# Moving two decay tiles of each group into the group ahead, the diagonal products behind a projection, and dt's sums behind another chunk

## The chip, the cores and the metric

The kernel runs on one core of a Trainium2 chip. A core has TensorE (matrix products, into PSUM), VectorE, ScalarE and GpSimd (POOL), which run their own instruction queues in order, and a SyncE queue (SP) whose only work here is to issue DMA transfers. The metric is the time of one execution in microseconds; lower is better.

## The reference, cut to what matters

Two layers run over 128 context tokens and 512 latent tokens: gated attention (layer 0), and a bidirectional Mamba-2 scan (layer 1), which the change touches. Of layer 1:

```
proj = h @ w_in                       # -> z, xbc, dt
xbc  = silu(conv3(xbc) + b)           # -> xs (2048), bs, cs (4 groups x 128)
dt   = softplus(dt + bias)            # 32 heads forward, 32 backward
a_cs = cumsum(a * dt)                 # within a chunk of 128 tokens; backward from the end
decay = exp(where(lower, a_cs[l] - a_cs[s], -inf))
y_diag = ((c @ b.T) * decay) @ (xs * dt)
states = b.T @ (xs * dt * exp(a_cs[-1] - a_cs))
h      = h * exp(a_cs[-1]) + states   # from chunk to chunk, both directions
y      = y_diag + (c @ h_prev) * exp(a_cs) + d_skip * xs
out    = rms_norm(y * silu(z)) @ w_out
```

There are 5 token tiles of 128 (tile 0 is the context, tiles 1 to 4 the latent tokens), and 32 heads in 4 groups of 8.

## The kernel before, in words

Layer 1 starts with a projection for dt (`dt_stage`, L917), a generator that is resumed between the first projections. Its first part projects; the second makes softplus on VectorE in a chain of small dependent operations that ends in L957 to L960; the third makes the running sums with two small products (L966, L967) and a total (L972); the fourth transposes the sums (L982) and stores them to DRAM in 40 small DMAs, one for each tile, group and direction (L990), and their exponential in one (L994).

Then `layer1` goes through 4 groups (g) of 10 steps (j). In a step stand the scan's operations of group g and, from the table `fl`, projections for what comes later. `x_unit` projects and convolves one chunk of 128 channels of xs for group g + 1 (48 products, L914, then VectorE's L1001, L1002, L1003, ScalarE's tanh L1005, VectorE's L1006), `bc_unit` does the same for B and C, `z_unit` projects a chunk of the gate path. `x_turn` and `b_turn` transpose a convolved chunk (L1014). In the last group, projections of the output (`part_mm`, L1380) stand in their place. A projection's result stands in the PSUM pool `pj`, which has two buffers; everything smaller takes one of the four buffers of the pool `pa`.

The decay of a tile t of group g takes four functions:

- `a_load` (L1121): two DMAs on SP spread the sums of 8 heads over 128 partitions, one for each direction, into tiles am0 (two buffers) and am1 (one buffer).
- `decay` (L1123): POOL masks both (L1125, L1126), ScalarE takes 16 exponentials (L1130), POOL adds the two directions into am0 (L1131). am1 is free from there.
- `mix` (L1133): TensorE multiplies B and C (L1136), VectorE multiplies the decay by that (L1137).
- `diag` (L1139): TensorE multiplies by xs (L1144), VectorE adds to Y (L1145). am0 is free when the products have read it.

`off` adds what the carried states give to Y (L1185 to L1187), with factors loaded by `e_load`; `advance` carries a state on (L1191 to L1195); `weighted` prepares its input on POOL (L1156); `state_init` transposes the loaded states (L1178). Y is one buffer, loaded at step 0 with d_skip * xs (`y_init`, L1116, from the tensor dud); `gate` multiplies it by the gate path at steps 6 and 9 (L1096), squares it (L1088, L1100) and stores it to yzd (L1101). In the code before, tiles are taken in the order 0, 2, 3, 1, 4:

```
if 1 <= j <= 5: mix(g, seq[j - 1])
if j == 0: a_load(g, seq[0])
if j < 5: decay(g, seq[j])
for t in {1: (0,), 3: (2, 3), 4: (1,), 5: (4,)}.get(j, ()): diag(g, t)
if j < 4: a_load(g, seq[j + 1])
for f in fl.get(j, []): f()
```

The order in which an engine runs its instructions is not that of the code. A planner orders them when the program is built: it plays the program through with its own estimates of durations, and whenever an engine is free there, takes the instruction that stands first in the code among those whose inputs and buffers are ready. The code's order is thus a priority. On the chip the order found is fixed, for SP's DMA issues too, and an instruction that isn't ready holds up all that is behind it on its engine.

Of the kernel before, what the change touches and what calls it, by code (L numbers as in the profile page):

```python
# [53 lines left out]
class Hybrid:  # L54
# [962 lines left out]
    def layer1(self, hT, wp, pj, pa, ctx):  # L1017
# [33 lines left out]
        def b_turn(g):  # L1051
            T = bcs[g]["T"]
            self.turn(bcs[g][0], pa, lambda t, ps: nc.scalar.copy(T[:, t, :], ps))
# [16 lines left out]
        def z_unit(g, jj):  # L1070
            zs, off_ = z_tile(g, jj)
            ps = self.proj_T(pj, wcur["z"], off_, P, hT)
            z_evac(zs, ps[:, 0:TW - 2])
# [44 lines left out]
        def a_load(g, t):  # L1118
            af = W[g, t] = [self.tl(wk, [P, 8, P], tag=f"am{d}", bufs=2 - d) for d in range(2)]
            for d in range(2):  # L1120
                nc.sync.dma_start(out=af[d].rearrange("p h l -> p (h l)"), in_=self.acd[t][g][d].rearrange("h l -> (h l)").unsqueeze(0).to_broadcast([P, 8 * P]))  # L1121

        def decay(g, t):  # L1123
            af = W[g, t]
            nc.gpsimd.affine_select(out=af[0], in_=af[0], pattern=[[0, 8], [1, P]], base=0, channel_multiplier=-1, compare_op=ALU.is_ge, fill=NEG)  # L1125
            nc.gpsimd.affine_select(out=af[1], in_=af[1], pattern=[[0, 8], [-1, P]], base=0, channel_multiplier=1, compare_op=ALU.is_ge, fill=NEG)  # L1126
            for d in range(2):
                for h in range(8):
                    i = 32 * d + 8 * g + h
                    nc.scalar.activation(af[d][:, h, :], af[d][:, h, :], AF.Exp, bias=self.nb[:, t, i:i + 1], scale=1.0)  # L1130
            nc.gpsimd.tensor_tensor(af[0], af[0], af[1], op=ALU.add)  # L1131

        def mix(g, t):  # L1133
            w = W[g, t][0]
            pc = self.tl(pa, [P, 512], tag="a")[:, 0:P]
            nc.tensor.matmul(pc, bcs[g][0][:, ts(t)], bcs[g][1][:, ts(t)], start=True, stop=True)  # L1136
            nc.vector.tensor_tensor(w, w, pc.unsqueeze(1).to_broadcast([P, 8, P]), op=ALU.mult)  # L1137

        def diag(g, t):  # L1139
            w = W.pop((g, t))[0]  # L1140
            pd = self.tl(pa, [P, 4, P], tag="a")
            for h in range(8):
                e = 64 * (h % 2)
                nc.tensor.matmul(pd[e:e + 64, h // 2, :], xts[g][:, t, HD * h:HD * h + HD], w[:, h, :], start=True, stop=True)  # L1144
            nc.vector.tensor_tensor(Y[:, t], Y[:, t], pd, op=ALU.add)  # L1145
# [23 lines left out]
        def state_load(g, d):  # L1169
            nme = "state_fwd_l1" if d == 0 else "state_bwd_l1"  # L1170
            st = St[g, d] = self.tl(wk, [P, 4, P], tag=f"st{d}", bufs=1)
            nc.sync.dma_start(out=st, in_=A[nme][0, 8 * g:8 * g + 8].rearrange("h p n -> (h p) n").rearrange("(j q) n -> q j n", q=P))
# [24 lines left out]
        def lag(f, g, j, before=None):  # L1197
            u = wcur.get("u")
            f(g, j)
            v = wcur["u"]  # L1200
            if before:
                wcur["u"] = u
                before[0](*before[1:])
                wcur["u"] = v
# [21 lines left out]
        lag(x_unit, 0, 0)  # L1226
        next(gen, None)
        lag(x_unit, 0, 1, (x_turn, 0, 0))
        next(gen, None)
        lag(x_unit, 0, 2, (x_turn, 0, 1))  # L1230
        next(gen, None)
        lag(x_unit, 0, 3, (x_turn, 0, 2))
        lag(bc_unit, 0, 0, (x_turn, 0, 3))
        lag(bc_unit, 0, 1, (b_turn, 0))
        for d in range(2):
            state_load(0, d)
        seq = [0, 2, 3, 1, 4]
        for g in range(NG):
            last = g == NG - 1
            nx = lambda jj: (lambda: lag(x_unit, g + 1, jj, (x_turn, g + 1, jj - 1) if jj else None))  # L1240
            zf = lambda jj: (lambda: z_unit(g, jj))
            if last:
                pt_ = lambda t, k: (lambda: part_turn(t, k))
                pm_ = lambda k: (lambda: part_mm(k))
                fl = {0: [zf(0), zf(1)], 1: [zf(2)], 2: [zf(3), pt_(2, 0), pt_(3, 0)], 3: [pt_(2, 1), pt_(3, 1), pm_(0)],
                      4: [pt_(2, 2), pt_(3, 2), pm_(2)], 5: [pm_(4)], 6: [pm_(6)], 7: [pm_(8)], 8: [pm_(10)]}
            else:
                fl = {j: [nx(j)] for j in range(4)}
                fl.update({4: ([zf(0)] if g else []) + [lambda: x_turn(g + 1, 3)], 5: [zf(1)] if g else [], 6: [lambda: bc_unit(g + 1, 0)], 7: [lambda: bc_unit(g + 1, 1)], 8: [zf(2), lambda: b_turn(g + 1)], 9: [zf(3)]})
            for j in range(10):  # L1250
                if 1 <= j <= 5:
                    mix(g, seq[j - 1])
                if 1 <= j <= 4:
                    for d in range(2):
                        off(g, j if d == 0 else 5 - j, d)
                if 1 <= j <= 3:
                    for d in range(2):
                        advance(g, j if d == 0 else 5 - j, d)
                if j in (4, 5):
                    prompt_state(g, j - 4)  # L1260
                if j == 0:
                    a_load(g, seq[0])
                    for d in range(2):
                        state_init(g, d)
                    for t in (0, 1, 4, 2, 3):
                        y_init(g, t)
                if j < 5:
                    decay(g, seq[j])
                for t in {1: (0,), 3: (2, 3), 4: (1,), 5: (4,)}.get(j, ()):
                    diag(g, t)  # L1270
                if j < 4:
                    a_load(g, seq[j + 1])
                    for d in range(2):
                        e_load(g, j + 1 if d == 0 else 4 - j, d)
                if j <= 2:
                    for d in range(2):
                        weighted(g, j + 1 if d == 0 else 4 - j, d)
                if j == 3:
                    for d in range(2):
                        weighted(g, 0, d)  # L1280
                for f in fl.get(j, []):
                    f()
                if last:
                    for t in {4: (2, 3), 5: (1, 0), 6: (4,)}.get(j, ()):
                        gate_last(t)
                        self.final_rstd(t, pa)
                    continue
                if j == 6:
                    gate(g, 0)
                    for d in range(2):  # L1290
                        state_load(g + 1, d)
                if j == 9:
                    gate(g, 1)
# [183 lines left out]
```

## Time and profile before

| | |
|---|---|
| median of 3 runs | 989.25 us (988.06 to 991.97) |
| the profiled execution | 989.37 us |
| its span, first to last instruction | 987.6 us |
| TensorE busy | 925.2 us |
| VectorE busy | 668.1 us |
| ScalarE busy | 516.3 us |
| POOL busy | 293.1 us |
| mean granted clock of TensorE | 0.981 |

Layer 1's projections begin at about 443 us; the groups' steps run from about 515 to 900 us; behind them come the remaining products of the output projection, to the end. A row of the timeline gives the start in us, the duration, the engine, the line, the operation, the tiles (written <- read) and how many instructions are merged; in brackets stands how long the engine was idle before it, and what it is taken to have waited for.

### The profile page before, as it was taken

Reading aid. Unit: us, or ns where it says so; the run is one execution under the profiler, and the core shown is the slowest. Engines: PE = TensorE matmul, PEld = TensorE weight load, DVE = VectorE, ACT = ScalarE, POOL = GpSimd, SP = SyncE. Lnnn points to the kernel's source line nnn. Section 1 sums busy time; section 2 is a strip of 40 time slices with the busy share of each in tenths; the row PEclk is TensorE's granted clock in tenths of the full one; section 3 lists DMA queues with packets and bytes.
Section 4 is the critical chain, followed back from the end, with each engine's and each line's share of the span. In section 5 each row is a group of like instructions: output and inputs, shape, how many; then the busy total and the mean of one; then the engine's idle time right before and its main releaser. Section 6 shows DMA issues by size and latency. Waiting matters only on the chain.

```text
span 987.6 us, 17414 instructions
## 1 busy us (share of the span) xinstructions
PE 925.2 (94%) x6578; PEld 842.7 (85%) x6578; DVE 668.1 (68%) x1112; ACT 516.3 (52%) x1208; POOL 293.1 (30%) x331
## 2 busy tenths in 40 slices
PE   5999999999999989999799988999999899899998
PEld 3898879879997779989699888999999899777886
DVE  4468666667685774784758765884597565797663
ACT  5346766666775753333436556456635562464340
POOL 3343213015060060140014355326332531353000
PEclk9999999999999999999899998999999999999999
DMA  9943324221113231333239674766475635455852
GB/s 312 352 141 101 103 96 139 74 67 43 32 39 125 86 107 68 126 127 105 79 97 289 175 213 153 217 179 219 129 212 162 217 107 185 155 166 195 284 186 92
DMA packets 121476, 146.98 MB, mean 149 GB/s; under 512 B 8688, under 2 KB 93808, under 8 KB 121392
## 3 DMA queue, kind: packets, MB, share of 16 engines
q1 hardware_dynamic: 110640, 140.62, 45.4%
q10 hardware_dynamic: 10752, 5.24, 1.8%
q8 instruction: 52, 0.85, 0.4%
q14 instruction: 32, 0.26, 0.1%
HBM read 128.73 MB, written 17.10 MB: 148 GB/s over the span
## 4 chain that ended last, share of the span: by engine, by line
PE 63%; DVE 11%; DMA 8%; ACT 6%; POOL 6%; issue 5%; SPq 1%; ACTq 0%; POOLq 0%; DVEq 0%
PE pj L914 17%; PE pp L283 8%; PE pj L1380 6%; DMA am<-acd 5%; PE a L841 4%; PE acc L379 3%; PE po L668 3%; ACT am L1130 3%; PE S L630 2%; PE pt L658 2%; PE a L1380 2%; PE pp L175 2%; DVE wl L74 2%; PE a L1185 2%; PE a L1191 2%
## 5 line engine op out<-in xcount | busy, mean ns | idle before, releaser
L914 PE MATMUL pj<-h,wh 128*128 128x322 f32 (+1 forms) x1248 | 293.4, 321 | 5.0 <-DVE B L1006 4.6
L914 PEld LDWEIGHTS pj<-h,wh 128*128 128x128 f32 (+1 forms) x1248 | 212.7, 191 | 14.2 <-issue 8.9
L914 PE MATMUL pj<-h,wl 128*128 128x322 f32 (+1 forms) x624 | 199.9, 320 | 0.0
L74 DVE TENSOR_TENSOR wl<-raw,wh 128x1024 fp32r<-128x1024 f32 (+1 forms) x113 | 128.2, 1147 | 55.6 <-ACT wh L73 53.0
L73 ACT CAST wh<-raw 128x1024 fp32r<-128x1024 f32 (+1 forms) x117 | 103.4, 912 | 102.5 <-PE pj L914 41.2
L1130 ACT ACTIVATE am<-am,nb 128x128 f32<-128x128 f32 x320 | 98.0, 390 | 76.7 <-POOL am L1126 50.8
L914 PEld LDWEIGHTS pj<-h,wl 128*128 128x128 f32 (+1 forms) x624 | 118.8, 190 | 3.3 <-issue 3.1
L283 PE MATMUL pp<-wh,big 128*128 128x256 f32 x576 | 111.9, 284 | 1.2 <-ACT sg L527 1.2
L283 PEld LDWEIGHTS pp<-wh,big 128*128 128x128 f32 x576 | 91.2, 188 | 1.4 <-ACT sg L527 1.4
L283 PE MATMUL pp<-wl,big 128*128 128x256 f32 x288 | 80.9, 281 | 0.0
L74 DVE TENSOR_TENSOR pl<-pt,ph 128x512 fp32r<-128x512 f32 (+1 forms) x100 | 59.3, 599 | 23.2 <-ACT ph L73 22.6
L637 ACT ACTIVATE Pt<-S,nm 128x640 f32<-128x640 f32 x64 | 51.2, 801 | 16.3 <-PE pt L658 12.5
L73 ACT CAST ph<-pt 128x512 fp32r<-128x512 f32 (+1 forms) x100 | 51.4, 517 | 15.3 <-PE pt L658 11.3
L1131 POOL TENSOR_TENSOR am<-am,am 128x1024 f32<-128x1024 f32 x20 | 48.6, 2428 | 35.6 <-ACT am L1130 35.6
L1156 POOL TENSOR_TENSOR xw<-xt,ws 128x512 f32<-128x512 f32 x32 | 34.6, 1099 | 80.5 <-ACT xt L1040 61.5
L633 DVE TENSOR_REDUCE nm<-S 128x1 f32<-128x640 f32 x64 | 52.4, 819 | 8.9 <-PE S L630 8.1
L283 PEld LDWEIGHTS pp<-wl,big 128*128 128x128 f32 x288 | 54.3, 188 | 0.0
L630 PE MATMUL S<-kT,qT 128*128 128x320 f32 x256 | 51.2, 324 | 2.7 <-ACT Pt L637 2.6
L658 PE MATMUL pt<-cst,Pt 128*128 128x128 f32 x320 | 51.0, 276 | 2.8 <-DVE pl L74 1.8
L1380 PE MATMUL pj<-wh,h 128*128 128x512 f32 x160 | 51.6, 398 | 0.0
L89 POOL TENSOR_SCALAR qss<-qss 128x4 f32<-128x4 f32 x25 | 6.3, 252 | 141.6 <-DVE qss L472 115.1
L1125 POOL TENSOR_SCALAR_AFFINE_SELECT am<-am 128x1024 f32<-128x1024 f32 x20 | 26.1, 1307 | 72.3 <-DMA am<-acd 54.7
(345 smaller groups left out, 2072.3 us busy)
## 6 DMA issues: line engine op xcount, KB each, us to landing
raw<-in_l_w_in SPq DMA_DIRECT2D x48, 512.0 KB
am<-acd SPq DMA_DIRECT2D x40, 512.0 KB
raw<-in_l_w_out SPq DMA_DIRECT2D x36, 512.0 KB
og<-in_l_mod_w SPq DMA_DIRECT2D x29, 512.0 KB
E<-ecd SPq DMA_DIRECT2D x64, 128.0 KB
raw<-in_l_w_in SPq DMA_DIRECT2D x25, 256.0 KB
mw<-in_l_mod_w SPq DMA_DIRECT2D x11, 512.0 KB
ys<-dud SPq DMA_DIRECT2D x20, 256.0 KB
```

Source lines behind the costliest of these rows:

```text
L73: (heng.tensor_copy if heng else self.nc.scalar.copy)(hi, src)
L74: (eng or self.nc.vector).tensor_tensor(lo, src, r32(hi), op=ALU.subtract)
L283: nc.tensor.matmul(ps, a[:, k, cs], b[:, k, :], start=k == 0 and a is hi and b is w[0], stop=k == KD - 1 and a is lo)
L630: nc.tensor.matmul(S[:, 192 + 320 * q:512 + 320 * q], qTs[g, t][:, h, :], kT[:, hl, 320 * q:320 * q + 320], start=hl == 0, stop=hl == 1)
L633: nc.vector.tensor_reduce(c["m"], c["s"], axis=AX.X, op=ALU.max, negate=True)
L637: nc.scalar.activation(Pt, c["s"], AF.Exp, bias=c["m"], scale=1.0, accum_out=rss[g][t][:, h:h + 1])
L658: nc.tensor.transpose(pt[:, 2 * i + j, :], Pts[j][:, kt * P:kt * P + P], self.ident)
L841: self.nc.tensor.matmul(ps, self.ohl[a][:, k, ts], w[b][:, k, :], start=k == 0 and i == 0, stop=k == KD - 1 and i == 2)
L914: nc.tensor.matmul(ps[0:m, 190 + 322 * half:512 + 322 * half], w[b][:, k, off:off + m], hT[s][:, k, 322 * half:322 * half + 322], start=fi ...
L1130: nc.scalar.activation(af[d][:, h, :], af[d][:, h, :], AF.Exp, bias=self.nb[:, t, i:i + 1], scale=1.0)
L1131: nc.gpsimd.tensor_tensor(af[0], af[0], af[1], op=ALU.add)
L1380: nc.tensor.matmul(self.PS[t][n], y[a][:, kk, :], b, start=k0 + k == 0 and i == 0, stop=k0 + k == 15 and i == 2)
```

## The change

The loads and the decays of tiles 0 and 2 of a group move to steps 6 and 8 of the group ahead (for group 0, ahead of the second half of B and C); those of tiles 3, 1 and 4 stand at steps 1, 2 and 4, each load beside its decay. `mix` of the five tiles stands at steps 0, 1, 3, 4 and 5, and `diag` in the same step, behind the step's projections instead of ahead of them. Before the groups, the third part of `dt_stage` (the sums) is resumed behind the third chunk's projection and the second chunk's transposition, and the fourth part directly behind it.

```diff
--- before.py
+++ after.py
@@ -1226,15 +1226,18 @@
         lag(x_unit, 0, 0)
         next(gen, None)
         lag(x_unit, 0, 1, (x_turn, 0, 0))
+        lag(x_unit, 0, 2, (x_turn, 0, 1))
         next(gen, None)
-        lag(x_unit, 0, 2, (x_turn, 0, 1))
         next(gen, None)
         lag(x_unit, 0, 3, (x_turn, 0, 2))
         lag(bc_unit, 0, 0, (x_turn, 0, 3))
+        for t in (0, 2):
+            a_load(0, t)
+            decay(0, t)
         lag(bc_unit, 0, 1, (b_turn, 0))
         for d in range(2):
             state_load(0, d)
-        seq = [0, 2, 3, 1, 4]
+        mixed = {0: 0, 1: 2, 3: 3, 4: 1, 5: 4}
         for g in range(NG):
             last = g == NG - 1
             nx = lambda jj: (lambda: lag(x_unit, g + 1, jj, (x_turn, g + 1, jj - 1) if jj else None))
@@ -1248,8 +1251,8 @@
                 fl = {j: [nx(j)] for j in range(4)}
                 fl.update({4: ([zf(0)] if g else []) + [lambda: x_turn(g + 1, 3)], 5: [zf(1)] if g else [], 6: [lambda: bc_unit(g + 1, 0)], 7: [lambda: bc_unit(g + 1, 1)], 8: [zf(2), lambda: b_turn(g + 1)], 9: [zf(3)]})
             for j in range(10):
-                if 1 <= j <= 5:
-                    mix(g, seq[j - 1])
+                if j in mixed:
+                    mix(g, mixed[j])
                 if 1 <= j <= 4:
                     for d in range(2):
                         off(g, j if d == 0 else 5 - j, d)
@@ -1259,17 +1262,14 @@
                 if j in (4, 5):
                     prompt_state(g, j - 4)
                 if j == 0:
-                    a_load(g, seq[0])
                     for d in range(2):
                         state_init(g, d)
                     for t in (0, 1, 4, 2, 3):
                         y_init(g, t)
-                if j < 5:
-                    decay(g, seq[j])
-                for t in {1: (0,), 3: (2, 3), 4: (1,), 5: (4,)}.get(j, ()):
-                    diag(g, t)
+                for gt in (((g, {1: 3, 2: 1, 4: 4}[j]),) if j in (1, 2, 4) else ((g + 1, {6: 0, 8: 2}[j]),) if j in (6, 8) and not last else ()):
+                    a_load(*gt)
+                    decay(*gt)
                 if j < 4:
-                    a_load(g, seq[j + 1])
                     for d in range(2):
                         e_load(g, j + 1 if d == 0 else 4 - j, d)
                 if j <= 2:
@@ -1280,6 +1280,8 @@
                         weighted(g, 0, d)
                 for f in fl.get(j, []):
                     f()
+                if j in mixed:
+                    diag(g, mixed[j])
                 if last:
                     for t in {4: (2, 3), 5: (1, 0), 6: (4,)}.get(j, ()):
                         gate_last(t)
```

## Rows read from the trace of the kernel before

**Rows 1.** The page, busy us by engine, share of the span, instructions
```profile
PE 925.2 (94%) x6578; PEld 842.7 (85%) x6578; DVE 668.1 (68%) x1112; ACT 516.3 (52%) x1208; POOL 293.1 (30%) x331
```

**Rows 2.** Windows: stretch, length, busy by engine (instructions), granted clock, DMA share, GB/s
```profile
480.70:487.40 6.70, 0.01 (x1) 0.00 (x0) 6.33 (x12) 1.99 (x2) 0.00 (x0) 0.83 0.13 45
485.20:491.90 6.70, 4.43 (x17) 3.75 (x17) 3.91 (x10) 4.44 (x8) 0.00 (x0) 0.50 0.12 38
550.00:553.30 3.30, 3.30 (x14) 3.30 (x13) 3.27 (x5) 1.53 (x6) 2.54 (x2) 0.50 0.91 273
...
853.80:857.10 3.30, 3.30 (x25) 2.32 (x23) 3.30 (x5) 1.09 (x3) 0.00 (x0) 0.50 0.63 210
...
875.00:900.00 25.00, 21.32 (x109) 16.83 (x110) 24.01 (x33) 12.12 (x17) 15.22 (x18) 1.00 0.58 192
```

**Rows 3.** Timeline of TensorE, at its longest waits in layer 1
```profile
487.47 0.90 PE L966 MATMUL a<-am,xs 128*128 128x160 f32 x2 [6.75 <-DVE am L960]
...
548.76 0.77 PE L1014 MATMUL a<-cst,u 128*128 128x128 f32 x5 [2.04 <-DVE u L1006]
...
587.75 0.66 PE L1144 MATMUL a<-am,xt 128*64 128x128 f32 x3 [3.17 <-ACT ym L1165]
...
602.06 0.63 PE L914 MATMUL pj<-h,wh 128*128 128x322 f32 x1 [2.98 <-DVE B L1006]
...
780.28 0.98 PE L1144 MATMUL a<-am,xt 128*64 128x128 f32 x14 [2.93 <-DVE am L1137]
...
802.15 0.39 PE L914 MATMUL pj<-h,wh 128*128 128x322 f32 x1 [1.07 <-DVE B L1006]
...
853.39 1.67 PE L1144 MATMUL a<-am,xt 128*64 128x128 f32 x16 [2.91 <-issue]
```

**Rows 4.** Timeline of POOL, additions of two decays and one mask
```profile
584.05 2.35 POOL L1131 TENSOR_TENSOR am<-am,am 128x1024 f32<-128x1024 f32 x1 [2.63 <-ACT am L1130]
...
592.40 2.08 POOL L1126 TENSOR_SCALAR_AFFINE_SELECT am<-am 128x1024 f32<-128x1024 f32 x1
...
796.64 2.42 POOL L1131 TENSOR_TENSOR am<-am,am 128x1024 f32<-128x1024 f32 x1 [2.64 <-ACT am L1130]
```

**Rows 5.** The chain that ended last, in time: start, us, what
```profile
489.97 1.07 PE a L1014 x5
...
602.06 17.23 PE pj L914 x96
...
802.15 14.54 PE pj L914 x96
...
830.38 1.05 PE a L1144 x16
```

**Rows 6.** Groups by line and form: busy us, mean ns, idle before and releasers
```profile
L1130 ACT ACTIVATE am<-am,nb 128x128 f32<-128x128 f32 x320 | 98.0, 390 | 76.7 <-POOL am L1126 50.8 <-POOL am L1125 25.8
...
L1126 POOL TENSOR_SCALAR_AFFINE_SELECT am<-am 128x1024 f32<-128x1024 f32 x20 | 22.8, 1141 | 74.2 <-DMA am<-acd 74.2
```

**Rows 7.** Timeline of VectorE around dt's chain
```profile
480.97 0.94 DVE L1001 TENSOR_SCALAR u<-pj,cw,cols 128x641 f32<-128x641 f32 x1 [0.41 <-DMA dud<-u]
...
486.92 0.49 DVE L960 SCALAR_TENSOR_TENSOR am<-am,xs 128x320 f32<-128x320 f32 x1
```

**Rows 8.** Timeline of ScalarE at the boundary of groups 0 and 1
```profile
597.40 2.44 ACT L1130 ACTIVATE am<-am,nb 128x128 f32<-128x128 f32 x8
...
600.46 0.69 ACT L1005 ACTIVATE pj<-B 128x641 f32<-128x641 f32 x1
```

**Rows 9.** Timeline of SP, the queue of DMA issues, at the same boundary
```profile
599.74 12.55 SPq L1121 DMA_DIRECT2D am<-acd  x2
```

**Rows 10.** Timeline of VectorE at the start of group 2
```profile
722.09 0.69 DVE L1187 TENSOR_TENSOR ys<-ys,a 128x512 f32<-128x512 f32 x1 [0.48 <-DMA ys<-dud]
...
725.15 0.81 DVE L1006 SCALAR_TENSOR_TENSOR u<-pj,u 128x641 f32<-128x641 f32 x1
...
728.25 0.94 DVE L1001 TENSOR_SCALAR u<-pj,cw,cols 128x641 f32<-128x641 f32 x1 [1.09 <-PE pj L914]
```

## The prediction

> **What bounds the kernel now.** I read the page's engine shares first: TensorE is busy for 94% of the span [rows 1], so a reordering can win only where TensorE stands still or runs slowly. Then I asked for the waits of TensorE, looked at each on the timeline, and asked the windows behind each for the granted clock. In layer 1 from 480 us on the reader is to see a short list. (a) Before the running sums of dt (L966) TensorE is idle 6.75 us, and the clock then stands at 0.50, the 1.2 GHz level, for the next 6.7 us [rows 2, 3]. (b) At 548.76 it waits 2.04 us to transpose, until VectorE has finished the convolution. (c) At 587.75 it waits 3.17 us for a diagonal product; the wait is put down to a PSUM buffer, but the POOL addition of that tile's decay ends at 586.40 (584.05 + 2.35) [rows 4] and VectorE's multiplication comes behind it, so I take the decay as the cause. (d) At 602.06 a projection waits 2.98 us for its PSUM buffer. (e) 2.93 us at 780.28 for a mixed tile, (f) 1.07 us at 802.15 as in (d), (g) 2.91 us at 853.39 before the products of tiles 2 and 3 of group 3 [rows 3]. After (b), (c) and (g) the windows show 0.50 for 3.3 us each (the first and the last of the three stand there) [rows 2]; after (d) two projections take 17.23 us, where the same two one boundary later take 14.54 us [rows 5]. (h) From 875 to 900 TensorE is busy for 21.32 of 25 us while VectorE is busy for 24.01 [rows 2]. All else is dense. With the half of each stretch at 0.50 these come to some 36 us; they are the target, not the time of any engine.
>
> **The change part by part.** No instruction is added or removed: the same 20 tiles, each two loads, two POOL masks (1.14 us each), 16 exponentials (98.0 us over 20 tiles, 4.9 us each), one POOL addition (2.35 us), one multiplication and 16 matmuls (1.05 us) [rows 4, 5, 6]. Only the program order changes, which is the planner's priority. Every term is therefore a wait.
>
> dt's sums. The projection that the change puts ahead of the sums is ahead of them already: VectorE starts its convolution at 480.97, when TensorE has finished it, and the sums wait for VectorE's dt chain, whose last product starts at 486.92 [rows 7]. What moves is the transposition of the chunk before (1.07 us, now behind the sums [rows 5]); at half clock that is worth 0.5 us. The bounds are 0 and 6.75 + 3.35 = 10.1 us (idle time, and half of 6.7 us at 0.50), the latter if the planner also finds something to put there; a loss would need a longer dt chain, and nothing is added to it. I take 0.5, the end that the rows are near to, as the next projection still has lower priority than the sums.
>
> Two tiles in the group ahead. In the code before, tiles 0 and 2 of the next group come last in priority, but the planner makes them early all the same: the addition of group 3's tile 2 runs at 796.64, before the projection at 802.15 behind which that group's steps begin [rows 3, 4]. What is late is the use: group 3's first product is at 830.38 [rows 5], and until then both buffers of tag am0 are full, so tiles 3, 1 and 4 can't be loaded. The change mixes tile 0 at step 0 and multiplies at its end, and tile 2 at step 1, which frees the two buffers one to two projections earlier (7.3 us each, 14.54 / 2 [rows 5]). Tile 4's buffer comes free one projection later than now, as tile 3's product goes behind it, but its own product moves behind a projection too. So the late decays (c) and (e) lose their waits: (c) 3.17 + 3.3/2 = 4.8 us, (e) 2.9 us. Moving the products behind each step's projection or output product puts such work between the advance of the states and the product in (g): 2.91 + 1.65 = 4.6 us.
>
> Half effects. (d) and (f) come from ScalarE: eight exponentials of the next group's tile run from 597.40 to 599.84 and the tanh of the convolution only at 600.46 [rows 8]. The change gives these exponentials a higher priority than the convolution, but spreads them over steps 6 and 8; (d) is worth 2.98 + 2.69 = 5.7 us, (f) 1.1 us, and I count half of each, 2.9 and 0.5. (b) is VectorE's order, worth 2.04 + 1.65 = 3.7; half is 1.9. In (h) 3.7 us are missing; tiles mixed earlier relieve VectorE there, half is 1.8.
>
> New waits. The moved loads go on SP ahead of weight loads, and a load whose buffer isn't free holds up all behind it: at 599.74 SP's two am loads stretch over 12.55 us [rows 9]. TensorE didn't notice then, since weights are loaded a pair of projections (14.54 us) ahead; without that cover it would be 12.55. On POOL the moved masks stand ahead of the squares' additions, on ScalarE ahead of casts. The early product of tile 0 needs Y, which is one buffer: its initial load waits for the store of the group before, and already now VectorE waits 0.48 us for it at 722.09 [rows 10]. None of this is measured with the new order; it is bounded by zero and by one SP hold (12.55) per boundary, three in all, 38 us. I take one wait like (d) and one like (b), 5.7 + 3.7 = 9.4 us, being what the present order pays in its first group.
>
> The sum: 0.5 + 4.8 + 2.9 + 4.6 = 12.8 us, halves 2.9 + 0.5 + 1.9 + 1.8 = 7.1, less 9.4: 10.5 us. The profiled execution took 989.37 us, so 978.9; the median of the runs shown is 0.1 lower, which gives 978.8.
>
> One row speaks against making decays beside the gating of the group ahead: a mask took 2.08 us at 592.40 against a mean of 1.14 [rows 4, 6], and VectorE was multiplying from SBUF at about that time. The Trainium skill, "SBUF — State Buffer", section "Who interferes with whom", says that a VectorE instruction with two SBUF inputs and a GpSimd instruction that reads SBUF take turns on a shared port, the later one blocked for the other's whole run. The trace agrees, with 0.94 us for that mask. By the rule two tiles in three boundaries, three POOL instructions each, would pay up to 18 × 0.94 = 17 us on POOL or VectorE, an estimate; on TensorE the sum would change only where that engine is the one waited for, and most of these tiles stand beside the gating already, so I leave it as it is.
>
> **The rivals.** *The planner had it all already.* For it speaks that tiles 0 and 2 are made ahead and that the projection is before the sums. Against it, that the program order still sets when a tile is mixed. Then only (c) and dt's half microsecond remain, 5.3 us, less one new wait as long as (b)'s 2.0: 3.3 us, so 986.0.
>
> *Everything closes.* The dt gap is filled as well: 12.8 + 7.1 + 9.6 (the rest of dt's 10.1), less the same 9.4 of new waits, is 20.1, so 969.2. For it speaks that all the gaps are between work that exists elsewhere; against it, that the planner's times differ from the chip's, which is how the present gaps came about.
>
> *Slower: Y isn't there.* The product of tile 0 is added to Y at step 0, one projection earlier than now. VectorE runs in order. If the planner puts that addition in VectorE's queue at about 717 in group 2, and Y lands at 722.09 [rows 10], VectorE stands 5.1 us with the convolution behind it. The convolution's last operation now ends at 725.96 (725.15 + 0.81 [rows 10]), 2.3 us before TensorE is through with the next projection (728.25, when the following convolution starts, released by it). Above 2.3 us the hold reaches TensorE: 2.8 us and 1.65 us of half clock, 4.4 in each of three groups, 13.3. In that case the later tiles are pushed back as well and only (c) and dt are won, 5.3: 989.3 - 5.3 + 13.3 = 997.3. Against it: in group 0 Y is there long before, and the planner counts loads too.
>
> **How the numbers follow.** Likeliest (0.52): 978.8, own range 970 to 984. Planner had it (0.20): 986. All closes (0.12): 969. Slower (0.16): 997. Half a per cent, 4.9 us, is about what a measurement of this kernel tells from no change: faster is below 984.3, slower above 994.2. Faster 0.50 + 0.12 = 0.62; same 0.02 + 0.20 = 0.22; slower 0.16. The range runs from 966 to 994: some 5% lie below, some 15% above.
>
> **What would show it.** Right: no wait at the sites of (c), (e) and (g); tile 0's product about one projection after the state transposes in each group, tile 1's addition some 10 to 20 us earlier within its group. The dt gap still 5 us or more. Wrong: VectorE waiting over 2.3 us for ys from dud; ScalarE's tanh behind exponentials at all three boundaries, with TensorE waiting over 3 us at each; weights landing late behind an am load on SP. The prediction fails as a whole if the planner's new order opens waits at sites that I haven't named.

## The result, and the profile after

The changed kernel takes 1000.0 us (median of 8, 994.4 to 1001.6) against 989.1 us for the one before (8 executions beside it): a ratio of 1.0093, with a 95% interval of 1.0068 to 1.0119. It is slower by some 9 to 11 us, where 978.8 was forecast. Its profiled execution took 998.5 us, with a span of 996.7 us.

The page's engine line, columns as in [rows 1]:

```profile
PE 926.2 (93%) x6578; PEld 839.9 (84%) x6578; DVE 678.6 (68%) x1112; ACT 516.8 (52%) x1208; POOL 302.6 (30%) x331
```

The work is the same, yet VectorE is busy 10.5 us longer and POOL 9.5 us longer than in [rows 1]: the same instructions took longer. TensorE's busy time is 1.0 us more, its share about a per cent less: TensorE stood still 8.1 us longer (the spans differ by 9.1). Where it stood is told best by a view that groups TensorE's waits by what ended them (line, who released it: total us, times, longest). First the kernel before, from 540 to 905 us:

```profile
PE pj L914 <- DVE B L1006: 4.6, 3, 3.0
PE a L1144 <- ACT ym L1165: 3.2, 1, 3.2
PE a L1144 <- DVE am L1137: 2.9, 1, 2.9
PE a L1144 <- issue: 2.9, 1, 2.9
PE pj L1380 <- DVE wl L74: 2.3, 3, 1.3
PE a L1014 <- DVE u L1006: 2.0, 1, 2.0
PE a L1385 <- POOL ssq L1108: 1.8, 2, 1.6
```

The same view of the changed kernel:

```profile
PE a L1014 <- DVE u L1006: 6.7, 5, 2.8
PE pj L914 <- DVE B L1006: 5.4, 3, 3.6
PE pj L914 <- DVE zs L1068: 4.5, 2, 4.2
PE a L1144 <- issue: 2.4, 1, 2.4
PE a L1185 <- ACT xt L1040: 2.2, 1, 2.2
PE a L1387 <- POOL ssq L1108: 1.8, 2, 1.5
PE a L1144 <- ACT ym L1165: 1.4, 1, 1.4
PE a L1185 <- DVE h L1195: 0.3, 1, 0.3
```

This pair is the result in small. The rows of L1144, the products of decayed tiles (three before, two after), fall from 9.0 to 3.8 us: the change does what it says. The rows released by a convolution or a gate chunk (L1006, L1068) rise from 6.6 to 16.6 us, and the sum of all rows from 19.7 to 24.7. Waits for decays were traded for waits on the projections' own evacuation (VectorE's reading of their results out of PSUM), at a loss.

The waits that answer to [rows 3], on TensorE's timeline of the changed kernel:

```profile
485.56 0.87 PE L966 MATMUL a<-am,xs 128*128 128x160 f32 x2 [6.04 <-issue]
557.38 1.16 PE L1185 MATMUL a<-B,h 128*128 128x128 f32 x8 [2.19 <-ACT xt L1040]
564.48 0.74 PE L1014 MATMUL a<-cst,u 128*128 128x128 f32 x5 [2.76 <-DVE u L1006]
578.14 0.55 PE L1144 MATMUL a<-am,xt 128*64 128x128 f32 x6 [1.37 <-ACT ym L1165]
594.25 0.88 PE L914 MATMUL pj<-h,wh 128*128 128x322 f32 x2 [3.55 <-DVE B L1006]
...
647.45 0.87 PE L1014 MATMUL a<-cst,u 128*128 128x128 f32 x3 [1.95 <-DVE u L1006]
708.45 0.54 PE L914 MATMUL pj<-h,wh 128*128 128x322 f32 x2 [1.45 <-DVE B L1006]
749.91 0.73 PE L1014 MATMUL a<-cst,u 128*128 128x128 f32 x5 [1.31 <-DVE u L1006]
796.27 0.87 PE L914 MATMUL pj<-h,wh 128*128 128x322 f32 x2 [4.17 <-DVE zs L1068]
...
866.70 0.84 PE L1144 MATMUL a<-am,xt 128*64 128x128 f32 x11 [2.36 <-issue]
```

Against [rows 3], site (e) is gone, (c) and (g) are shorter, (a), (b) and (d) stand. New are 557, 647, 708, 749 and 796. The windows (columns as in [rows 2]) show what such a wait costs afterwards:

```profile
558.65:562.06 3.41, 3.07 (x4) 0.67 (x2) 2.86 (x5) 3.41 (x10) 1.35 (x1) 0.50 0.74 220
565.47:568.88 3.41, 3.41 (x23) 3.08 (x19) 3.41 (x5) 1.67 (x5) 1.34 (x1) 0.50 0.76 212
592.78:599.61 6.83, 5.36 (x20) 5.39 (x21) 5.80 (x6) 5.97 (x14) 6.81 (x4) 0.50 0.36 107
647.39:650.80 3.41, 3.35 (x16) 3.38 (x17) 2.90 (x4) 1.48 (x3) 0.88 (x1) 0.50 0.39 136
794.17:801.00 6.83, 4.73 (x18) 4.76 (x19) 5.92 (x7) 4.03 (x13) 4.60 (x6) 0.50 0.83 250
```

In these five, 23.9 us together, the granted clock is 0.50, the 1.2 GHz level. Before, there were three stretches of some 3.4 us (two of them in [rows 2]) and one of 6.83 behind (d), 17.1 us. At most half of the difference, 3.4 us, is lost to it. TensorE also stands still in these stretches, and by its busy time in them (19.9 us against 15.9 before) the loss is 2.0 us. With the 5.0 us of waits that is 7.0 of the 9.1 us between the two spans. Another 1.7 us of standing lies behind 905 us, where the kernel before has none. One gain is whole: no half clock is left around site (g), the granted clock from 820 to 880 us being 1.00.

How a wait behind late exponentials comes about is seen at 594, where [rows 3] had site (d). ScalarE's timeline in the changed kernel:

```profile
587.72 4.93 ACT L1130 ACTIVATE am<-am,nb 128x128 f32<-128x128 f32 x16 [5.96 <-POOL am L1126]
592.56 0.69 ACT L1005 ACTIVATE pj<-B 128x641 f32<-128x641 f32 x1
```

VectorE's, for the chunk whose tanh that is:

```profile
584.28 0.89 DVE L1003 SCALAR_TENSOR_TENSOR B<-pj,cw,B 128x641 f32<-128x641 f32 x1
...
593.28 0.83 DVE L1006 SCALAR_TENSOR_TENSOR B<-pj,B 128x641 f32<-128x641 f32 x1 [5.05 <-ACT pj L1005]
```

POOL's, with the mask that holds the exponentials:

```profile
586.15 1.53 POOL L1126 TENSOR_SCALAR_AFFINE_SELECT am<-am 128x1024 f32<-128x1024 f32 x1 [3.00 <-DMA am<-acd]
```

And SP's, with the load that holds the mask:

```profile
580.16 1.31 SPq L1121 DMA_DIRECT2D am<-acd  x2
```

Read from the bottom: the loads go out at 580.16 to 581.47, the mask gets its data at 586.15, 4.7 us or more after its load; ScalarE has stood 5.96 us in front of the exponentials, runs 16 of them, and only then takes the tanh, whose input had been ready since 585.17 (584.28 + 0.89). It starts 7.4 us late, VectorE's last step of the convolution with it, and TensorE waits 3.55 us for the PSUM buffer, with the clock at 0.50 from 592.78 to 599.61. From 540 to 905 us VectorE's waits for that tanh (L1006 and L1187, released by L1005) are 12.3 us before and 19.6 us after.

Of the five new sites only two came about in this way. At 557 ScalarE has stood 6.21 us in front of eight exponentials (from 554.41) for a mask that waited for its load, and behind them comes the copy that TensorE waits for. At 708 it has stood 3.22 us in front of eight (from 704.40), and behind them comes the tanh at 706.76. At 647 the tanh is over in time, at 644.08, and VectorE is never idle ahead of its last step:

```profile
644.20 2.37 DVE L1194 TENSOR_TENSOR h<-h,cd 128x512 f32<-128x512 f32 x1
646.49 0.81 DVE L1006 SCALAR_TENSOR_TENSOR u<-pj,u 128x641 f32<-128x641 f32 x1
647.22 0.68 DVE L1194 TENSOR_TENSOR h<-h,cd 128x512 f32<-128x512 f32 x1
```

What is late is L1194, which takes 2.37 us, where the same product takes 0.68 us a little later. POOL, at the same time:

```profile
643.64 2.38 POOL L1131 TENSOR_TENSOR am<-am,am 128x1024 f32<-128x1024 f32 x1 [0.78 <-ACT am L1130]
```

At 749 it is the same: L1194 takes 2.30 us from 746.73, beside an addition from 746.08 to 748.48. At 796 VectorE first stands 9.08 us for another load (its row is shown below the list of gains), and then has long rows beside POOL as well. So the late loads are directly ahead of 3.6 of the 11.1 us that TensorE stands at the new sites, and VectorE's long rows beside POOL, at 796 together with the other load, are ahead of the other 7.4.

### The profile page after: what moved, and what is told of

Read it like the earlier page. It is cut to its first block, busy times and chain, and to the rows that moved or that the text cites. A ratio compares the mean times of both kernels' runs of the same rounds, so it can differ in the third digit from the quotient of the medians.

```text
span 996.7 us, 17430 instructions
## 1 busy us (share of the span) xinstructions
PE 926.2 (93%) x6578; PEld 839.9 (84%) x6578; DVE 678.6 (68%) x1112; ACT 516.8 (52%) x1208; POOL 302.6 (30%) x331
## 5 line engine op out<-in xcount | busy, mean ns | idle before, releaser
L914 PE MATMUL pj<-h,wl 128*128 128x322 f32 (+1 forms) x624 | 197.9, 317 | 0.5 <-DVE wl L74 0.5
L74 DVE TENSOR_TENSOR wl<-raw,wh 128x1024 fp32r<-128x1024 f32 (+1 forms) x113 | 130.0, 1162 | 41.0 <-ACT wh L73 38.2
L74 DVE TENSOR_TENSOR pl<-pt,ph 128x512 fp32r<-128x512 f32 (+1 forms) x100 | 59.4, 599 | 23.1 <-ACT ph L73 22.5
L73 ACT CAST ph<-pt 128x512 fp32r<-128x512 f32 (+1 forms) x100 | 51.5, 518 | 15.3 <-PE pt L658 11.3
```

What stands on the lines that cost most here:

```text
L73: (heng.tensor_copy if heng else self.nc.scalar.copy)(hi, src)
L74: (eng or self.nc.vector).tensor_tensor(lo, src, r32(hi), op=ALU.subtract)
L914: nc.tensor.matmul(ps[0:m, 190 + 322 * half:512 + 322 * half], w[b][:, k, off:off + m], hT[s][:, k, 322 * half:322 * half + 322], start=fi ...
```

## The experiments

All times are medians beside runs of the kernel before on the same chip (its medians there: 989.1 to 989.7 us), with the ratio to it and its 95% interval.

### Which part of the change

`dt_only`, on the kernel before:

```diff
         lag(x_unit, 0, 1, (x_turn, 0, 0))
+        lag(x_unit, 0, 2, (x_turn, 0, 1))
         next(gen, None)
-        lag(x_unit, 0, 2, (x_turn, 0, 1))
         next(gen, None)
```

> The kernel before with only dt's sums moved (the third part resumed behind the third chunk's projection and the second chunk's transposition, the fourth part directly behind it). A, the sums are not the cause: the gap ahead of the sums stood at 6.75 us before and 6.04 us after, so 989 within 2 us. B, moving the sums shifts everything behind them in the planner's order and is itself the loss: 995 to 1001. The prediction had priced this part at a gain of 0.5 us.

Measured: 989.0 us, 0.9991 (0.9971 to 1.0010). The sums cost and give nothing; A holds.

`decays_only` is the changed kernel with that diff undone.

> The changed kernel with dt's sums resumed where they were, so only the decays and the diagonal products are moved. A, the decays and their places are the cause: 998 to 1002, as the changed kernel's 1000.0. B, the sums are the cause: 989 to 991.

Measured: 997.6 us, 1.0085 (1.0055 to 1.0116), just under what A said: the loss is in the decays and products. The 11 executions lie between 991.8 and 1006.4 us, and the profiled one is the lowest, so its trace is not read here.

`place_only`, on the kernel before:

```diff
-                for t in {1: (0,), 3: (2, 3), 4: (1,), 5: (4,)}.get(j, ()):
-                    diag(g, t)
...
-                    a_load(g, seq[j + 1])
...
                 for f in fl.get(j, []):
                     f()
+                if 1 <= j <= 5:
+                    diag(g, seq[j - 1])
+                if j < 4:
+                    a_load(g, seq[j + 1])
```

> The kernel before with only the diagonal products moved: each still in the steps 1 to 5, but alone and behind the step's projections; loads and decays stay in the steps 0 to 4, each load behind the product that frees its buffer. D, the place of the products is the cause (they hold am0 and a PSUM buffer of pool pa longer): 995 to 1001. E, the early decays are the cause: 987 to 991; the wait of 2.91 us ahead of the products of tiles 2 and 3 in group 3 goes, as the prediction said of site (g), which is worth 4.6 us at most.

Measured: 996.4 us, 1.0077 (1.0055 to 1.0100). The run moves the loads of a later tile along with the products, as the diff shows, so it isn't the products' place alone that it tries.

`early_only`, on the changed kernel:

```diff
-        mixed = {0: 0, 1: 2, 3: 3, 4: 1, 5: 4}
+        mixed = {1: 0, 2: 2, 3: 3, 4: 1, 5: 4}
...
+                if j in mixed:
+                    diag(g, mixed[j])
                 for gt in ...
...
-                if j in mixed:
-                    diag(g, mixed[j])
```

> The changed kernel with the products in the steps 1 to 5, one in each, ahead of the step's decay and projections: only the loads and decays of tiles 0 and 2 are early. E, the early decays are the cause: 996 to 1001, with the waits on zs near 790 and on B near 594 that the changed kernel has. D: 988 to 991. If both this and the kernel with moved products alone are at 989, the two together are needed for the loss.

Measured: 994.9 us, 1.0057 (1.0039 to 1.0075). That is between what D and E said, and neither holds alone: each half loses by itself, 7.1 and 5.5 us. (In this run the decays of tiles 3 and 1 stand a step earlier too, as in the change.) In TensorE's waits of `place_only` the trade is plainest:

```profile
PE a L1014 <- DVE u L1006: 6.3, 3, 2.8
PE pj L914 <- DVE B L1006: 4.8, 3, 3.7
...
PE pj L914 <- DVE zs L1068: 2.6, 1, 2.6
PE pj L1381 <- DVE xt L1068: 1.5, 1, 1.5
```

No wait for a decayed tile is left (9.0 us before), and the four rows of L1006 and L1068 make 15.2 us (6.6 before). But all rows of this view together come to 21.0 us, 1.3 more than before, while its span is 8.4 us longer; for `early_only` they come to 18.9 us, less than before, with a span 5.5 us longer. So the view shows the trade, and not where these two runs lose their time.

### Four other suspects

`decays_behind`, on the changed kernel:

```diff
-        for t in (0, 2):
-            a_load(0, t)
-            decay(0, t)
         lag(bc_unit, 0, 1, (b_turn, 0))
+        for t in (0, 2):
+            a_load(0, t)
+            decay(0, t)
...
                 for f in fl.get(j, []):
                     f()
+                if j in (6, 8) and not last:
+                    a_load(g + 1, {6: 0, 8: 2}[j])
+                    decay(g + 1, {6: 0, 8: 2}[j])
```

> The changed kernel with the moved decays behind the projection of their step: those of steps 6 and 8 behind the step's fl entries, group 0's first two behind the second half of B and C. S, ScalarE's order is the cause (exponentials of the next group's tile, queued ahead of a tanh whose input is ready, while POOL's masks hold them up): the first group lost 6.8 us there, the wait of 3.55 us on a projection's buffer with 6.8 us at half clock near 594 goes, and the time falls to 990 to 994. P, contention of POOL with VectorE for SBUF is the cause: the same POOL work runs beside the same gating, 998 to 1001. Y, the late Y: unchanged, 1000.

Measured: 999.5 us, 1.0097 (1.0063 to 1.0131). S failed as put. ScalarE's timeline shows that the tanh is behind the 16 exponentials all the same:

```profile
589.60 4.79 ACT L1130 ACTIVATE am<-am,nb 128x128 f32<-128x128 f32 x16 [6.86 <-POOL am L1126]
594.29 0.68 ACT L1005 ACTIVATE pj<-B 128x641 f32<-128x641 f32 x1
```

The code order is only a priority, and here it did not bring the tanh ahead of the exponentials. So the run didn't try what it was meant to, and doesn't clear ScalarE.

`diag0_late`, on the changed kernel:

```diff
+                if j == 1:
+                    diag(g, 0)
                 for gt in ...
...
-                if j in mixed:
+                if j in mixed and j:
                     diag(g, mixed[j])
```

> The changed kernel with tile 0's diagonal product taken from the end of step 0 to step 1, ahead of that step's decay; everything else as changed. Y, VectorE held at tile 0's addition by the load of Y is the cause (3.15, 0.94 and 1.34 us of holds in the groups 1 and 2, with a convolution behind them): VectorE no longer waits for ys from dud and the time falls by 4 to 8 us, to 992 to 996. S or P: 999 to 1001.

Measured: 1000.3 us, 1.0098 (1.0073 to 1.0124). VectorE's waits for ys from dud, 5.4 us in the changed kernel, fell to 0.4 us, and the time did not move. But the waits moved again: TensorE's rows of L1006 and L1068 fell from 16.6 to 9.5 us, those of L1144 rose from 3.8 to 6.9, and all rows together came to 24.3 us, against 24.7. So the holds for Y are there, as the slower rival said; taking them away alone gives nothing back, and that they have no share in the loss is not shown.

`noadd_before` and `noadd_after` leave out POOL's addition in each kernel:

```diff
-            nc.gpsimd.tensor_tensor(af[0], af[0], af[1], op=ALU.add)
```

> The kernel before with POOL's addition of the two directions left out (the decay is the forward half alone, 20 additions of 2.35 us, 47 us of POOL, are gone). It is the base for the next. P, contention of POOL with VectorE: VectorE's prolonged instructions (17 us over the nominal durations between 480 and 905 us) fall to 10 or less, time 984 to 988. Without contention: 986 to 990, from site (c) alone.

> The changed kernel with the same addition left out. P, contention is the cause of the loss: VectorE's prolongation (29 us in the changed kernel) falls to that of the one without the change, and the difference between the two without additions is under 4 us. Q, queues in order (ScalarE's exponentials ahead of a tanh, Y, buffers): the difference stays 7 to 12 us.

Measured: 984.8 us, 0.9946 (0.9928 to 0.9964), and 997.5 us, 1.0086 (1.0052 to 1.0120). The difference is 12.7 us, no smaller than with the addition. Single rows do show VectorE and POOL in each other's way, as L1194 at 644.20 beside the addition at 643.64. That is what the Trainium skill, "SBUF — State Buffer", section "Who interferes with whom", describes for a VectorE instruction with two inputs in SBUF and a GpSimd instruction that reads SBUF. The trace agrees: L1194 ends at 646.57, 0.55 us behind the addition. It explains part of the longer busy times. Without the addition VectorE is busy for 660.5 us in the changed kernel and 664.1 in the other: its extra 10.5 us are gone, and the loss is not. So the longer rows stand ahead of three of the new sites, but they are not the cause of the whole.

`mirror_before` and `mirror_after` take the two scan directions in the other order in all seven loops:

```diff
-                    for d in range(2):
+                    for d in (1, 0):
...
-                    for t in (0, 1, 4, 2, 3):
+                    for t in (0, 4, 1, 3, 2):
```

> The kernel before with the two scan directions taken in the other order within each step (backward first, in all seven loops over the direction, and Y's loads in that order): the same work, the same places of decays and products. L, the code order of the kernel before is a lucky one among equals, and any reordering pays some new waits: 993 to 1000. C, the loss belongs to what the change does: 987 to 991.

> The changed kernel with the two directions swapped in the same way. C: 997 to 1002, and the difference from the mirrored kernel before is 8 to 12 us. L: anywhere from 988 to 1002, and the difference from the mirrored kernel before is under 5 us.

Measured: 990.7 us, 1.0016 (0.9997 to 1.0036), and 999.4 us, 1.0105 (1.0075 to 1.0136). A difference of 8.7 us: C holds, and in this one other order, too, the change loses.

### The decay's front half

`noscal_before` and `noscal_after`, on each kernel:

```diff
-            nc.gpsimd.affine_select(out=af[0], ...)
-            nc.gpsimd.affine_select(out=af[1], ...)
             for d in range(2):
-                for h in range(8):
-                    i = 32 * d + 8 * g + h
-                    nc.scalar.activation(af[d][:, h, :], af[d][:, h, :], AF.Exp, bias=self.nb[:, t, i:i + 1], scale=1.0)
+                nc.scalar.activation(af[d], af[d], AF.Exp)
```

> The kernel before with the decay's masks left out and its 16 exponentials with a bias for each head replaced by one for each direction without one (so the decays' values are others): POOL loses 40 masks, 46 us, and ScalarE most of 98 us. It is the base for the next. S, ScalarE's order: the waits for a tanh held behind exponentials go, 978 to 986. Without S: 984 to 990.

> The changed kernel with the same left out. S, ScalarE held by masks and exponentials is the cause of the loss: the difference between the two kernels without them is under 3 us. R, the cause lies elsewhere (VectorE's order, Y, buffers of PSUM and of am0): it stays 7 to 13 us.

Measured: 987.7 us, 0.9980 (0.9960 to 1.0000), and 991.3 us, 1.0025 (1.0000 to 1.0049). The difference falls to 3.6 us, a little above what S said: most of the loss goes through the masks or the exponentials. The kernel before gained only some 1.5 us, to 987.7, where S had said 978 to 986.

`oneexp_before` and `oneexp_after` take only the second part of that diff, the exponentials.

> The kernel before with loads and masks as they are, but one exponential for each direction in place of 8 (without bias, so the decays' values are others): ScalarE loses some 70 of its 516 us. Base for the next. U: 980 to 986. T: 986 to 990.

> The changed kernel with the same single exponentials. U: the difference between the two is under 4 us. T, a late load holds ScalarE just as long, however short the exponentials are: 7 to 12 us.

Measured: 991.8 us, 1.0013 (0.9994 to 1.0031), and 995.6 us, 1.0057 (1.0035 to 1.0080). The difference is 3.8 us, as U said, where T had said 7 to 12. But U had also said that the kernel before would get faster, to 980 to 986, and it did not: with 54 us taken off ScalarE (516.3 to 462.6 us busy) it stands still, and the changed one gains 4.5 us (the intervals of its two ratios overlap). By these runs the exponentials' length counts in the changed kernel's order and not in the other.

`noload_before` and `noload_after` leave out the loads of the spread sums:

```diff
-            for d in range(2):
-                nc.sync.dma_start(out=af[d]..., in_=self.acd[t][g][d]...)
...
-            nc.gpsimd.affine_select(out=af[0], in_=af[0], ...)
+            nc.gpsimd.affine_select(out=af[0], in_=self.ident.unsqueeze(1).to_broadcast([P, 8, P]), ...)
...
-                    nc.scalar.activation(..., bias=self.nb[:, t, i:i + 1], scale=1.0)
+                    nc.scalar.activation(..., bias=self.zero, scale=1.0)
```

> The kernel before without the 40 loads of the sums' spreads into am0 and am1 (the masks read the identity, the exponentials take no bias, so the decays' values are others; masks, 16 exponentials and the addition of each tile stay). Base for the next. T, the lateness of the loads is what holds POOL's masks, then ScalarE's exponentials, then the tanh behind them: 982 to 987. Otherwise 986 to 990.

> The changed kernel without the same loads. T: the difference between the two kernels without loads is under 3 us, as it was (3.6) without masks and single exponentials. U, the exponentials' own time on ScalarE (4.9 us a tile), ahead of convolutions that they stand in front of, is the cause: it stays 7 to 12 us.

Measured: 975.5 us, 0.9857 (0.9828 to 0.9887), and 972.3 us, 0.9821 (0.9794 to 0.9847). The first is lower than either theory said. This is the pair that turns the sign: with masks, all exponentials and POOL's addition in place, the changed kernel is 3.2 us below the other (the intervals overlap, so no worse is what is shown). TensorE's waits in it, 540 to 905 us:

```profile
PE a L1014 <- DVE u L1006: 2.2, 1, 2.2
PE pj L914 <- DVE B L1006: 1.4, 1, 1.4
PE a L1385 <- POOL ssq L1108: 1.3, 1, 1.3
PE a L1183 <- DVE ys L1185: 0.8, 1, 0.8
PE pj L1380 <- ACT h L73: 0.7, 1, 0.7
```

6.4 us in all (7.8 in the kernel before without loads), none at L1144's counterpart, and VectorE's waits for the tanh are 2.3 us where the changed kernel has 19.6. The exponentials are as many and as long, and still run ahead of a tanh (eight from 579.35, the tanh at 581.71); but they no longer stand waiting in front of it. That this wait is what cost the time is the likeliest reading, not the only one. Every kernel here has an order planned for itself, and the loads' traffic is gone as well (DMA share 0.47 from 540 to 905 us, against 0.58), so the size of the gain in each kernel, 14 and 28 us, is not the price of lateness alone.

`ampool_after` and `ampool_before` issue the same loads from POOL:

```diff
-                nc.sync.dma_start(out=af[d]...
+                nc.gpsimd.dma_start(out=af[d]...
```

> The changed kernel with the 40 loads of am0 and am1 issued from POOL in place of SP; same data, buffers and code order. H, the loads' place in SP's queue is the cause (SP stood 88.8 us of the stretch from 540 to 905 us at these loads for a buffer, 63.5 us before the change, with weights, E, Y and the next loads behind them): SP no longer stands at them, and the time falls to 985 to 994. T alone, the loads come as late as before for want of a free am1 or am0, whoever issues them: 996 to 1002.

> The kernel before with the same loads issued from POOL. H: faster than before, 980 to 987, and the changed kernel with loads from POOL within 4 us of it. T alone: 988 to 994, and the difference between the two stays 7 to 12 us. A wait of POOL for am0's buffer, with its masks and the weighting behind it, could also make either slower than with SP.

Measured: 995.7 us, 1.0071 (1.0046 to 1.0095), and 987.1 us, 0.9971 (0.9952 to 0.9989). That SP stands at these loads is real. SP's waits at these loads, first in the kernel before, from 540 to 905 us (columns as for TensorE):

```profile
SPq L1121 <- POOL am L1131: 40.4, 11, 6.9
SPq L1121 <- PE a L1144: 23.1, 13, 3.3
```

In the changed kernel:

```profile
SPq L1121 <- POOL am L1131: 56.3, 16, 6.3
SPq L1121 <- PE a L1144: 32.5, 13, 6.1
```

These are waits for the single am1 buffer (its addition) and for am0 (its products), 25 us longer after the change. With the loads on POOL, SP has none of them. Both kernels come out a little below what T alone gave them, so the hold was worth some 2 to 4 us to each. But the difference between them stays at 8.6 us, so H is refuted as the cause of the loss, and T is left: the loads are late whoever issues them. T alone isn't the whole, since short exponentials took most of the difference away too. The kernel before is faster by 0.3% with loads from POOL.

## Why the prediction was wrong, point by point

The step that failed is the one under "New waits": "I take one wait like (d) and one like (b), 5.7 + 3.7 = 9.4 us". In the profiled execution the five new sites cost 2.19 + 1.95 + 1.45 + 1.31 + 4.17 = 11.1 us of standing, and the half clock behind those at 557, 647 and 796 at most another (3.41 + 3.41 + 6.83) / 2 = 6.8: 17.9 us (16.6 by TensorE's busy time in these stretches). That is inside the bounds given there (0 to 38), but 7 to 8.5 above the value chosen. The prediction priced the new order by what the old one pays in its first group. Of the ways in which the new waits came about it had named one, "ScalarE's tanh behind exponentials"; the other, VectorE held beside POOL, it had priced at up to 17 us and left out of the sum, and that stands ahead of 7.4 of the 11.1 us. By its own last sign, waits at sites that it hadn't named, it fails as a whole.

The gains were the other half of the miss, 12.8 + 7.1 = 19.9 us forecast. From the rows:

- dt's sums: 6.75 to 6.04 us, 0.7 in the trace, where 0.5 was said; alone they move nothing that can be measured. Right.
- (c): 3.17 to 1.37 us, and the 0.50 stretch behind it gone, 3.5 us of 4.8. (e): 2.93 us gone, as said, but not its origin. In the kernel before, VectorE stands 9.0 us for an early load of the output projection's input (u from yzd), and behind it comes the multiplication that (e) waits for, at 779.02; in the changed kernel it stands as long, and behind it come the gating, two conversions of weights and the zs that TensorE waits for at 796 (rows below this list). (g): 2.91 to 2.36 us, and its half clock gone, 2.2 of 4.6; the product still waits with "issue" as the releaser, and that cause was never found.
- The halves: (f) is gone, 1.1 for 0.5. (b) has its counterpart at 564.48 with 2.76 us for 2.04, (d) at 594.25 with 3.55 for 2.98: together 1.3 us worse, where 4.8 was counted. In (h), the waits at L1380 for L74 are gone from the list (2.3 us), where 1.8 was said.
- Sum: 0.7 + 3.5 + 2.9 + 2.2 + 1.1 - 1.3 + 2.3 = 11.4 us.

The two holds of VectorE, first in the kernel before, then in the changed one:

```profile
777.74 1.36 DVE L1369 TENSOR_TENSOR u<-u,cols 128x512 f32<-128x512 f32 x1 [8.98 <-DMA u<-yzd]
```

```profile
787.30 0.69 DVE L1371 TENSOR_TENSOR u<-u,cols 128x512 f32<-128x512 f32 x1 [9.08 <-DMA u<-yzd]
...
788.63 2.53 DVE L1096 TENSOR_TENSOR ys<-ys,zs 128x512 f32<-128x512 f32 x1
791.08 4.31 DVE L74 TENSOR_TENSOR wl<-raw,wh 128x1024 fp32r<-128x1024 f32 x2
```

The last two rows are long: in the kernel before two L1096 take 1.29 us at 784.31, and two L74 2.35 us at 780.15. In the changed kernel POOL adds from 788.20 and is busy almost without a break to 795.7.

So 7 to 8.5 us too few new waits and 8.5 too much gain make some 16 to 17 of the 19.6 us between 978.9 and 998.5; the rest lies in waits under 1 us, ahead of 540 and behind 905 us.

What was right: tile 0's product now comes about one projection after the state transposes in the first three groups (L1144 at 620.52, L1178 at 612.41; in the last it is 15.3 us). The fourth addition of a group, tile 1's by the code's order, comes 18 to 33 us earlier, counted from the state transposes, where 10 to 20 was said. So the decays did move as far as they should, and further. The dt gap is still over 5 us. Of the signs that were to show it wrong, VectorE waited 3.15 us for ys from dud, and TensorE 3.55 us behind a late tanh, but over 3 us at one of the boundaries, not at all three. Of the rivals, "The planner had it already" is refuted, since tiles do become free earlier; "everything closes" too. "Slower: Y isn't there" gave 997.3, near the result, but by a mechanism that the run with a late tile 0 doesn't bear out: its holds went, and the time stayed. Of the estimate of up to 17 us on POOL or VectorE, at most 10.5 and 9.5 us were to be seen as longer busy times of VectorE and POOL. Leaving it out of the sum left a part of the new waits unpriced (647, 749, 796); yet the pair without POOL's addition lost no less, so pricing it alone would not have given the loss.

The cause, as far as it is shown, lies in the front half of the moved decays: a decay is a chain of load, mask, exponentials and addition through one am1 buffer and two of am0. Its middle stands on ScalarE, in the order that the planner found by its own durations, ahead of convolutions and copies. On the chip POOL and ScalarE stand waiting for the loads (traced at 557, 594 and 708), and what they hold up is no longer a decayed tile with time to spare, but a tanh or a copy that frees TensorE's PSUM buffer. Without the loads the loss is gone; with short exponentials a third to a half of it is left (3.8 of 10.9 us, 0.44 of 0.93% by the ratios); without SP's hold, without POOL's addition, without the wait for Y, or with the directions swapped nearly all of it is there or more (8.6 to 12.7 us).

What stays open: how the late loads make up the whole loss, when only two of the five new sites in the trace have them directly ahead; no run tells whether the additions that stand beside VectorE at the others came there by the same lateness. Open is which part of the loads' lateness, the wait for a buffer or the time to land, makes the difference between the two orders. A second am1 would tell, but it would have to take its 4 KB of each partition from other tiles, and wasn't tried. Open too is why the order with moved products (and loads) loses by itself, with the decays where they were; its waits in the view are of the same kind, but make up only 1.3 us of its 8.4, and no run took the loads out of that order.

## What to carry to other kernels

When work is moved earlier, ask of each engine that it crosses what will stand behind it there if its input is late: a late load in front of a tile with slack can cost nothing, and here it cost 3.55 us and a stretch at half clock in front of a tanh that frees TensorE's next buffer. Ask, too, what will run beside it. Price "new waits" by the number of places where moved work stands in front of or beside such an operation (five new ones here), not by one sample of each kind in the old order. And where a planner orders the work by its own durations, taking the uncertain input away, as the pair without loads did, says more than several changes of the code's order, though the input's traffic goes with it.

## What the runs showed of the hardware that was not expected

Issuing one of these loads took POOL 0.53 to 0.60 us (34 of them from 540 to 905 us in the kernel before with loads from POOL), and SP 0.32 us at the least and 0.34 in the median (35 of them in the kernel before). Though POOL itself then stands for buffers at such loads, once for 6.67 us, that kernel is 0.3% faster as a whole. A VectorE product of two tiles in SBUF took 2.37 and 2.30 us beside a POOL addition, against 0.68, and twice that reached TensorE, which waited 1.95 and 1.31 us behind it. And executions of one program can differ more than these kernels do: 991.8 to 1006.4 us for the decays alone, 985.1 to 995.6 us for the kernel before in 22 executions. A single trace of such a kernel shows how a wait comes about, not what it costs on the whole; the sums over sites above hold for the two executions that were traced.
